# Block inversion in a hybrid decoder block: the order of the fp16 products on TensorE

## The chip, the core and the metric

The kernel runs on one core of a Trainium2 chip. The metric is the device time of one execution in microseconds (us). The engines of the core are written as in the profile: PE is TensorE's matmul side, PEld its weight loads, DVE is VectorE, ACT is ScalarE, POOL is GpSimd, SP is SyncE, which issues most transfers. Each engine works through its own queue in program order, and waits for the others at semaphores.

## The reference

One decoder layer over 512 tokens of width 2048. A projection of the normed input feeds two branches, RWKV-7 time mixing and sliding-window attention, which are gated, merged and followed by a gated ConvFFN. What matters here is the time mixing: each of 16 heads keeps a 64x64 state and updates it token by token.

```python
def step(state, inp):
    r_t, k_t, v_t, w_t, ka_t, kb_t = inp
    sa = jnp.einsum('bhvk,bhk->bhv', state, ka_t)
    state = (state * w_t[:, :, None, :] + sa[..., None] * kb_t[:, :, None, :]
             + v_t[..., None] * k_t[:, :, None, :])
    y = jnp.einsum('bhvk,bhk->bhv', state, r_t)
    return state, y
```

## The kernel before

The recurrence is computed in chunks of 64 tokens: 8 chunks, and the 16 heads in 8 pairs (two heads fill 128 partitions). Inside a chunk the updates `sa` depend on one another through a strictly triangular 64x64 matrix, so the kernel inverts a unit triangular matrix for each head and chunk. `late(p, st)` does this for pair p by block doubling: the loop over `LEVELS[1:]` takes m = 2, 4, 8, 16, 32, and each level has two products for all 8 chunks, called here the **A product** (left side `AI`, the matrix itself, right side `X`, the inverse so far) and the **B product** (left side `BT`, the transposed inverse so far, right side `IW`, which is made of the A product's result).

The products run in fp16, and for the accuracy each side is split into a high part (rounded to fp16) and a low part (the rest). `mm3(ps, wt, both, hi)` makes one product: the left side's parts `wt[:, 0]` (high) and `wt[:, 1]` (low) are the loaded weights, `both(n)` streams the high and the low right part of chunk n side by side (64 columns), `hi(n)` the high right part alone (32 columns). So a product is 16 matmuls with 16 weight loads: high left times both (L673) and low left times high (L674) for each chunk. One PSUM bank takes all chunks; `added` sums its two halves.

Between the two products of a level stands a chain over ACT and DVE: ACT copies one half of the sum out of PSUM (L686), DVE adds the other half (L687), DVE applies a mask (L697), ACT rounds the result into the high right part and DVE subtracts it for the low right part (both in `split`, L209 and L210). After the B product it goes on with L686, L687, L711, L712, the new parts of X (ACT L714, DVE L715) and the transposes of X into `BT` (PE L719, copied out by ACT and DVE in L723, two copies on each).

After the five levels a chain over the 8 chunks carries the state: PE L731, copied by DVE L732; PE L734 (with the inverse `BX` as weights), copied by ACT L735 and DVE L736; PE L740; DVE L744 updates the state for the next chunk. Then the group norm of the result follows (DVE L758 to L765, with a square on ACT, L762), and `final`, which starts with the transposes of PE L772.

All that time PE has other work to place between: `early(p + 1)`, the next pair's first steps, and the gates. They need six projection tiles for each pair, and every tile is 48 matmuls of 128x512 (`project`, L255 to L257: high times high, high times low, low times high), called **z matmuls** below. Their weights come by DMA into a ring of four tiles, are rounded by ACT (`whi`, L240) and subtracted by DVE (`wlo`, L241); a place in the ring comes free when PE has used the load that lay there four loads before. Per pair there are 288 z matmuls in all. In which order each engine does all this is not written in the code: outside the calls marked with `pin`, a list scheduler orders each engine's queue from its own estimates of durations, and a small change in one place moves instructions on all engines.

Of the kernel before, what the change touches and what calls it, by code (L numbers as in the profile page):

```python
# [23 lines left out]
NCH = S // C  # L24
# [110 lines left out]
def block_kernel(ctx: ExitStack, tc: tile.TileContext, d: Dims, a: dict, out: bass.AP):  # L135
    nc = tc.nc
    act, dve, pool, pe, sync = nc.scalar, nc.vector, nc.gpsimd, nc.tensor, nc.sync
# [140 lines left out]
    if True:  # L278
# [3 lines left out]
        with tc.tile_pool(name="x0_ps", bufs=6, space=PSUM) as ps0:  # L282
# [10 lines left out]
            for h in range(2):  # L293
                hs = slice(h * HT * P, (h + 1) * HT * P)
                for k in range(NK):
                    ps = ps0.tile([P, HT * P], F32, name="ps_x", tag="x")
# [45 lines left out]
        with ExitStack() as pt:  # L342
# [4 lines left out]
            def small():  # L347
                return mps.tile([P, S], F32, name="mi", tag="mi")
# [26 lines left out]
            for t in range(NKV):  # L375
# [12 lines left out]
                ps = small().rearrange("p (n c) -> p n c", c=P)  # L388
                for b in range(NT):
                    pe.transpose(ps[:, b], vf[:, b * P : (b + 1) * P], ident)  # L390
                ps = ps.rearrange("p n (h c) -> p n h c", c=HD)
# [14 lines left out]
            for g in range(NHK):  # L406
# [7 lines left out]
                for n in range(NT):  # L414
# [32 lines left out]
                    for kb in kbs:  # L447
                        ps = small().rearrange("p (h c) -> p h c", c=P)
# [3 lines left out]
                    ps = small()  # L452
                    for kb in kbs:
                        for i in range(2):
                            pe.matmul(ps, vhl[:, n - 1 + kb, g].rearrange("p e c -> p (e c)"),
                                      phl[i][:, kb].rearrange("p h c -> p (h c)"),
                                      start=kb == kbs[0] and i == 0, stop=kb == kbs[-1] and i == 1)
                    ol = ap_.tile([HD, S], F32, name="ol", tag="ol", bufs=2)
                    act.activation(ol, ps[HD:P], AF.Copy)
                    ps, ol = (x[0:HD].rearrange("p (e j c) -> p e j c", e=2, c=P) for x in (ps, ol))  # L460
# [6 lines left out]
        with ExitStack() as pr:  # L467
# [21 lines left out]
            def bulk():  # L489
                return blk.tile([P, S], F32, name="bulk", tag="bulk")  # L490
# [105 lines left out]
            def late(p, st):  # L596
# [23 lines left out]
                for n0 in range(0, NCH, 2):  # L620
                    ps = bulk()
# [8 lines left out]
                for g in range(2):  # L630
# [7 lines left out]
                    ps = bulk().rearrange("p (n c) -> p n c", c=P)  # L638
# [11 lines left out]
                for g in range(2):  # L650
# [4 lines left out]
                    ps = bulk().rearrange("p (n c) -> p n c", c=P)  # L655
# [3 lines left out]
                ps = bulk().rearrange("p (t c) -> p t c", c=P)  # L659
# [10 lines left out]

                def mm3(ps, wt, both, hi):
                    for n in range(NCH):
                        pe.matmul(ps[:, n], wt[:, 0, n], both(n), start=True, stop=False)  # L673
                        pe.matmul(ps[:, n, 0], wt[:, 1, n], hi(n), start=False, stop=True)  # L674

                def halves(m, t):

# [2 lines left out]
                def level_sum():  # L680
                    return bulk().rearrange("p (n e c) -> p n e c", e=2, c=HC)
# [8 lines left out]
                for m in LEVELS[1:]:  # L690
                    last = m == LEVELS[-1]
                    ps = level_sum()
                    cols = [halves(m, X[:, e]) for e in range(2)]
                    mm3(ps, AI, lambda n: X[:, :, n].rearrange("p e (b w m) -> p e b w m", w=2, m=m)[:, :, :, 1],
                        lambda n: cols[0][:, n])
                    tt = added(ps)
                    dve.tensor_tensor(tt, tt, mb(f"m{m}", NCH), op=ALU.mult)  # L697
                    split(IW[:, :, 0], IW[:, :, 1], tt)
                    if last:
                        for i, (lo, hi) in enumerate(HV):  # L700
# [3 lines left out]
                            else:  # L704
                                act.activation(own, own, AF.Copy, scale=1.0 / SG)
                    ps = level_sum()
                    mm3(ps, BT, lambda n: IW[:, n], lambda n: IW[:, n, 0])
                    sc = 1.0 / (SG * SG) if last else 1.0 / SG
                    tt = added(ps)
# [3 lines left out]
                    if not last:  # L713
                        act.activation(cols[0], tv, AF.Copy, scale=sc)  # L714
                        dve.scalar_tensor_tensor(cols[1], tv, sc, cols[0], op0=ALU.mult, op1=ALU.subtract)  # L715
                        ps = blk.tile([P, 2, NCH // 2, P], F16, name="bulk", tag="bulk")
# [11 lines left out]
                for n in range(NCH):  # L728
                    ps = chn.tile([P, 2, C], F32, name="psG", tag="chn")
# [3 lines left out]
                    ps = chn.tile([P, 2, C], F32, name="psU", tag="chn")  # L733
# [5 lines left out]
                    for h in (1, 0):  # L739
                        pin(pe.matmul(s2[:, n % HN, h], W2[:, n, 2 * h : 2 * h + 2].rearrange("p a c -> p (a c)"), UV[:, n, h],  # L740
                                      start=True, stop=True))
# [124 lines left out]
    with ExitStack() as pbb:  # L866
# [8 lines left out]
        for m, i in order:  # L875
            hi, lo, r0, n, gi = parts[i]
# [509 lines left out]
```

## Time and profile before

| | |
|---|---|
| three runs, median (lowest to highest) | 2829.64 us (2828.12 to 2833.07) |
| the profiled execution's own time | 2830.7 us |
| its span, from first to last instruction | 2828.9 us |
| TensorE's granted clock, mean | 0.996 |
| PE busy, weight loads busy | 2774.4 us (98%), 2403.0 us (85%) |
| DVE, ACT, POOL busy | 1987.5, 1342.1, 225.1 us |
| stretch with the eight pairs, 340 to 1080 us: PE busy | 730.92 of 740 us |

A busy PE is counted from a matmul's start to the modelled end of it, and matmuls overlap; so what PE loses in a place is read best from the starts of two matmuls that follow each other. In an answer of the timeline each row has the start, the duration, engine, line, operation and operands; in square brackets stands the time that the engine was idle before it, and who released it.

### The profile page before, as it was taken

The numbers are of one execution on the slowest core, as the hardware profiler recorded it, in microseconds if no ns is written. First come the engines' busy times: TensorE is split into PE (matmuls) and PEld (weight loads), VectorE is DVE, ScalarE is ACT, GpSimd is POOL, SyncE is SP. The second block draws the span as 40 slices with busy tenths as digits, with TensorE's granted clock in tenths as the row PEclk, the third lists the DMA queues.
The fourth block names the chain that finished last, engine by engine and source line by source line (L and its number), as shares of the span: only waits on it lengthen the run. The fifth ranks groups of instructions, "written<-read, shape, count | busy, mean of one in ns | idle before, by whom it ended". The sixth has DMA issues, their size and how long they took to land.

```text
span 2828.9 us, 45923 instructions
## 1 busy us (share of the span) xinstructions
PE 2774.4 (98%) x17450; PEld 2403.0 (85%) x17450; DVE 1987.5 (70%) x3437; ACT 1342.1 (47%) x2256; POOL 225.1 (8%) x299
## 2 busy tenths in 40 slices
PE   7999999999999999999999899999999999999999
PEld 5777777777777777888888899999999999888887
DVE  4588677777777774545678777878787878655555
ACT  4355445444544553322465455555545555444444
POOL 0001000000000001011010011011101110000000
PEclk9999999999999999999999999999999999999999
DMA  7865766666666667878777789888988897877775
GB/s 216 227 159 163 187 167 168 175 164 158 175 162 171 160 165 223 234 248 292 237 251 211 210 235 241 229 229 227 241 236 222 228 242 228 315 245 241 256 256 190
DMA packets 223726, 607.04 MB, mean 215 GB/s; under 512 B 24448, under 2 KB 44560, under 8 KB 222480
## 3 DMA queue, kind: packets, MB, share of 16 engines
q1 hardware_dynamic: 156096, 432.64, 47.1%
q0 software_dynamic: 36064, 132.14, 24.5%
q10 hardware_dynamic: 31344, 39.31, 4.0%
q8 instruction: 137, 2.24, 0.3%
q14 instruction: 85, 0.70, 0.1%
HBM read 554.38 MB, written 174.40 MB: 258 GB/s over the span
## 4 chain that ended last, share of the span: by engine, by line
PE 87%; DVE 5%; ACT 3%; DMA 2%; issue 1%; SPq 0%; POOL 0%; ACTq 0%; DVEq 0%; POOLq 0%
PE X L1087 18%; PE X L954 11%; PE acc L256 9%; PE acc L255 9%; PE acc L257 9%; PE Y L954 9%; PE Y L1087 9%; PE Z L1087 4%; DVE wlo L241 1%; PE psS L740 1%; PE psG L731 1%; PE bulk L623 1%; PE bulk L673 1%; PE bulk L534 1%; ACT whi L240 1%
## 5 line engine op out<-in xcount | busy, mean ns | idle before, releaser
L255 PE MATMUL acc<-xhi,whi 128*128 128x512 f32 x1152 | 462.9, 402 | 1.9 <-DVE xlo L301 1.9
L257 PE MATMUL acc<-xhi,wlo 128*128 128x512 f32 x1152 | 463.8, 403 | 0.0
L256 PE MATMUL acc<-xlo,whi 128*128 128x512 f32 x1152 | 462.2, 401 | 0.0
L947 DVE TENSOR_TENSOR wlo<-raw,whi 128x1024 fp32r<-128x1024 f32 x210 | 256.9, 1224 | 205.1 <-ACT whi L946 204.9
L240 ACT ACTIVATE whi<-raw 128x512 fp32r<-128x512 f32 x352 | 220.0, 630 | 375.7 <-PE acc L256 295.1
L946 ACT ACTIVATE whi<-raw 128x1024 fp32r<-128x1024 f32 x210 | 222.8, 1061 | 290.6 <-PE X L954 152.9
L241 DVE TENSOR_TENSOR wlo<-raw,whi 128x512 fp32r<-128x512 f32 x352 | 241.3, 689 | 167.1 <-ACT whi L240 146.9
L1087 PE MATMUL X<-b,whi 128*128 128x256 f32 x1472 | 270.2, 284 | 2.3 <-DVE u L1107 0.9
L1087 PE MATMUL X<-t,whi 128*128 128x256 f32 x1408 | 259.6, 285 | 10.3 <-DVE u L1107 9.8
L1070 DVE TENSOR_TENSOR wlo<-raw,whi 128x1024 fp32r<-128x1024 f32 x176 | 215.0, 1222 | 77.6 <-ACT whi L1069 77.3
L1087 PE MATMUL Y<-t,whi 128*128 128x256 f32 x1408 | 257.1, 283 | 0.0
L255 PEld LDWEIGHTS acc<-xhi,whi 128*128 128x128 f32 x1152 | 217.6, 189 | 43.4 <-issue 2.5
L256 PEld LDWEIGHTS acc<-xlo,whi 128*128 128x128 f32 x1152 | 217.5, 189 | 41.9 <-issue 3.3
L257 PEld LDWEIGHTS acc<-xhi,wlo 128*128 128x128 f32 x1152 | 217.5, 189 | 38.3 <-issue 1.1
L1069 ACT ACTIVATE whi<-a 128x1024 fp32r<-128x1024 f32 x132 | 139.3, 1056 | 216.5 <-DVE a L1063 214.3
L1087 PEld LDWEIGHTS X<-b,whi 128*128 128x128 f32 x1472 | 230.7, 193 | 3.1 <-issue 2.4
L1087 PEld LDWEIGHTS X<-t,whi 128*128 128x128 f32 x1408 | 221.6, 194 | 10.9 <-DVE u L1107 7.2
L1087 PEld LDWEIGHTS Y<-t,whi 128*128 128x128 f32 x1408 | 219.8, 192 | 0.0
L1087 PE MATMUL X<-b,wlo 128*128 128x256 f32 x736 | 209.3, 284 | 2.1 <-DVE wlo L1070 2.1
L1070 DVE TENSOR_TENSOR wlo<-a,whi 128x1024 fp32r<-128x1024 f32 x132 | 161.7, 1226 | 67.3 <-ACT whi L1069 66.7
L1087 PE MATMUL X<-t,wlo 128*128 128x256 f32 x704 | 200.4, 285 | 0.0
L1087 PE MATMUL Y<-t,wlo 128*128 128x256 f32 x704 | 199.4, 283 | 0.0
(339 smaller groups left out, 5762.1 us busy)
## 6 DMA issues: line engine op xcount, KB each, us to landing
raw<-in_w_up_dram SPq DMA_DIRECT2D x180, 512.0 KB, 4.6
raw<-in_w_z_dram SPq DMA_DIRECT2D x288, 256.0 KB, 3.9
s_dn<-in_w_dn_dram POOLq DMA_DIRECT2D x88, 512.0 KB, 5.9
raw<-in_w_up_dram POOLq DMA_DIRECT2D x88, 512.0 KB, 8.7
raw<-s_dn SPq DMA_DIRECT2D x88, 512.0 KB, 3.8
raw<-in_w_dn_dram SPq DMA_DIRECT2D x66, 512.0 KB, 3.5
a<-in_w_up_dram SPq DMA_DIRECT2D x48, 512.0 KB, 6.9
s_dn<-in_w_dn_dram SPq DMA_DIRECT2D x44, 512.0 KB, 4.9
```

The source lines that it names most:

```text
L240: act.activation(hi, raw, AF.Copy)
L241: dve.tensor_tensor(lo, raw, hi.bitcast(F32), op=ALU.subtract)
L255: pe.matmul(acc, whi[:, j], xhi[:, k], start=first, stop=False)
L256: pe.matmul(acc, whi[:, j], xlo[:, k], start=False, stop=False)
L257: pe.matmul(acc, wlo[:, j], xhi[:, k], start=False, stop=last)
L534: pe.matmul(ps, w[:, i], ads[:, i], start=i == lo, stop=i == hi - 1)
L946: act.activation(whi, wr, AF.Copy)
L947: dve.tensor_tensor(wlo, wr, whi.bitcast(F32), op=ALU.subtract)
L954: pe.matmul(dst, l[:, q, ts], r[:, es], start=fst and j == 0, stop=lst and j == 2, skip_group_check=True)
L1069: pin(act.activation(hi, t, AF.Copy))
L1070: pin(dve.tensor_tensor(lo, t, hi.bitcast(F32), op=ALU.subtract))
L1087: pin(pe.matmul(ps, l[:, k], r[:, k], start=start and k + i == 0, stop=last and i == 2, skip_group_check=True))
```

## The change

The loop over the chunks is split in two. First come the low left parts of all chunks times the high right part, then the high left parts times both. The first matmul of the product alone starts the accumulation, the last alone ends it.

```diff
                 def mm3(ps, wt, both, hi):
                     for n in range(NCH):
-                        pe.matmul(ps[:, n], wt[:, 0, n], both(n), start=True, stop=False)
-                        pe.matmul(ps[:, n, 0], wt[:, 1, n], hi(n), start=False, stop=True)
+                        pe.matmul(ps[:, n, 0], wt[:, 1, n], hi(n), start=n == 0, stop=False, skip_group_check=True)
+                    for n in range(NCH):
+                        pe.matmul(ps[:, n], wt[:, 0, n], both(n), start=False, stop=n == NCH - 1, skip_group_check=True)
```

In the changed file the low part's matmul is L673, the high part's L675, and every line behind it has a number higher by one. The number of matmuls, weight loads and columns is the same. The scheduler lays the queues out anew from the first pair's first A product on until the end of the last pair's state chain; before and behind that nothing moves. The three places below are from the fourth pair.

On PE, the B product at m = 16, before: the last two z matmuls ahead of it and its first chunk (AI and BT are the left sides, XIW the tile with X and IW, xhi, xlo, whi and wlo the parts of the projection).

```order
L257 MATMUL acc<-xhi,wlo 128x512
L255 MATMUL acc<-xhi,whi 128x512
L673 LDWEIGHTS BT
L673 MATMUL bulk<-XIW,BT 128x64
L674 LDWEIGHTS BT
L674 MATMUL bulk<-XIW,BT 128x32
```

And now, from the last of its low parts to the first of its high parts:

```order
L673 LDWEIGHTS BT
L673 MATMUL bulk<-XIW,BT 128x32
L256 MATMUL acc<-xlo,whi 128x512
L257 MATMUL acc<-xhi,wlo 128x512
L675 LDWEIGHTS BT
L675 MATMUL bulk<-XIW,BT 128x64
```

Before, the 16 matmuls stand in one block; now two z matmuls stand between the eight low and the eight high ones. It is so in every B product, with one to three z matmuls (at m = 32 the four matmuls of L327 stand there as well). The numbers of z matmuls between the A product and the B product of a pair, for the second to the seventh pair at m = 2, 4, 8, 16, 32, were 17 (and 8 more inside the A product), 14, 15, 11, 15, and are 13 (and 9 inside the A product), 11, 10, 11, 9. At m = 2 the A product stood in three pieces and stands in two. Behind the B product they were 13, 10, 12, 10 and are 10, 11, 10, 10, until the transposes of L719. In the state chain they were 87 and are 90, from there to the next pair's first product 76 and 85. The blocks of z matmuls of a pair were 38 and are 41 (in the last pair 35 and 39).

The same level on ACT, before, between the two products (XIW<-tt is the split's high part):

```order
L723 COPY BT<-bulk 64x8x64
L686 ACTIVATE tt<-bulk 128x256
L723 COPY BT<-bulk 64x8x64
L209 ACTIVATE XIW<-tt 128x8x32
L240 ACTIVATE whi<-raw 128x512
```

And now:

```order
L724 COPY BT<-bulk 64x8x64
L687 ACTIVATE tt<-bulk 128x256
L724 COPY BT<-bulk 64x8x64
L240 ACTIVATE whi<-raw 128x512
L209 ACTIVATE XIW<-tt 128x8x32
```

The rounding of a z weight has moved ahead of the split's high part. On DVE, before:

```order
L723 COPY BT<-bulk 64x8x64
L687 TENSOR_TENSOR tt<-bulk,tt 128x256
L697 TENSOR_TENSOR tt<-tt,cst 128x256
L723 COPY BT<-bulk 64x8x64
L210 TENSOR_TENSOR XIW<-tt,XIW 128x8x32
L241 TENSOR_TENSOR wlo<-raw,whi 128x512
```

And now:

```order
L724 COPY BT<-bulk 64x8x64
L688 TENSOR_TENSOR tt<-bulk,tt 128x256
L698 TENSOR_TENSOR tt<-tt,cst 128x256
L724 COPY BT<-bulk 64x8x64
L241 TENSOR_TENSOR wlo<-raw,whi 128x512
L210 TENSOR_TENSOR XIW<-tt,XIW 128x8x32
```

The subtraction for that z weight has moved ahead of the split's low part. Both moves are there at m = 4, 8 and 16 in the second to the eighth pair, and in the eighth at m = 32. Behind the B product at m = 4, in the same way, a `whi` now stands ahead of L711 and L714 on ACT, and its `wlo` ahead of L715 on DVE; behind the one at m = 2 they stood there before. In the first pair the queues of the two engines between the products are as before, but for a `whi` at m = 32.

At the state chain's first chunk the small steps of the next pair's norm (rq) stood on DVE, before, partly behind the copy of L736:

```order
L198 TENSOR_TENSOR rq_7060<-rq_7059 128x8
L736 COPY UV<-psU 64x64
L199 TENSOR_TENSOR rq_7060<-rq_7060,rq_7058 128x8
L200 SCALAR_TENSOR_TENSOR rq_7059<-rq_7060,rq_7059 128x8
L198 TENSOR_TENSOR rq_7060<-rq_7059 128x8
L199 TENSOR_TENSOR rq_7060<-rq_7060,rq_7058 128x8
L744 SCALAR_TENSOR_TENSOR SV<-SV,ee,psS 64x64 x2
```

And now:

```order
L713 TENSOR_SCALAR BX<-tt 64x8x32
L198 TENSOR_TENSOR rq_7060<-rq_7059 128x8
L199 TENSOR_TENSOR rq_7060<-rq_7060,rq_7058 128x8
L200 SCALAR_TENSOR_TENSOR rq_7059<-rq_7060,rq_7059 128x8
L198 TENSOR_TENSOR rq_7060<-rq_7059 128x8
L199 TENSOR_TENSOR rq_7060<-rq_7060,rq_7058 128x8
L737 COPY UV<-psU 64x64
L200 SCALAR_TENSOR_TENSOR rq_7059<-rq_7060,rq_7059 128x8
```

Five of these steps now stand between L713 and the copy of L737 (L712 and L736 before), and four more between that copy and the state's update. PE has 3 z matmuls between L734 and L740 there as before. Between L740 and L731 it had 4, and now has 2, the transpose L330 and one matmul of L558.

## Prediction

> **What bounds the kernel now.** I read the page's first lines, then the stretch of the eight pairs, then who waits for whom on the weight loader.
>
> ```profile
> span 2828.9 us, 45923 instructions
> PE 2774.4 (98%) x17450; PEld 2403.0 (85%) x17450; DVE 1987.5 (70%) x3437; ACT 1342.1 (47%) x2256; POOL 225.1 (8%) x299
> 340.00:1080.00 740.00, 730.92 (x4848) 581.26 (x4847) 553.28 (x1339) 357.82 (x795) 59.68 (x81) 1.00 0.67 166
> PEld L673 <- DVE XIW L210: 23.3, 40, 1.0
> PEld L719 <- DVE XIW L715: 8.3, 30, 0.4
> ```
>
> PE is the bound: it is busy for 730.92 of the 740 us in which the change acts. Whatever is won or lost here is time in which PE starts nothing, or starts something late. All 40 B products (8 pairs, 5 levels) wait for the low right part. What such a wait costs is read from the starts, here in the fourth pair at m = 16: on PE the last matmul of the A product, the z matmuls, the first two of the B product, and the B product's first weight load.
>
> ```profile
> 662.63 0.18 PE L674 MATMUL bulk<-XIW,AI 128*128 128x32 f16 x1
> 662.66 0.48 PE L257 MATMUL acc<-xhi,wlo 128*128 128x512 f32 x1
> 662.98 0.40 PE L255 MATMUL acc<-xhi,whi 128*128 128x512 f32 x1
> ...
> 664.80 0.39 PE L257 MATMUL acc<-xhi,wlo 128*128 128x512 f32 x1
> 665.03 0.39 PE L255 MATMUL acc<-xhi,whi 128*128 128x512 f32 x1
> 665.34 0.20 PE L673 MATMUL bulk<-XIW,BT 128*128 128x64 f16 x1
> 665.38 0.18 PE L674 MATMUL bulk<-XIW,BT 128*128 128x32 f16 x1
> ...
> 665.33 0.10 PEld L673 LDWEIGHTS <-BT 128*128 128x128 f16 x1 [0.34 <-DVE XIW L210]
> ```
>
> A z matmul takes 0.23 from start to start (664.80 to 665.03), the first one behind fp16 work 0.32 (662.66 to 662.98), an fp16 matmul 0.03. The B product came 0.31 after the last z matmul, so PE lost 0.08, while the loader shows 0.34 of idle: 0.26 of that is there without a wait. So the 23.3 us stand for 23.3 - 40 x 0.26 = 12.9 us of PE, 1.6 for each pair, and the 8.3 at L719 for 8.3 - 30 x 0.26 = 0.5. These 12.9 us are the most that the change can take away. What the chain between the products does in the same place, on ACT and then on DVE:
>
> ```profile
> 662.42 0.58 ACT L723 COPY BT<-bulk 64x512 f16<-64x512 f16 x1 [0.51 <-PE bulk L719]
> 662.90 0.38 ACT L686 ACTIVATE tt<-bulk 128x256 f32<-128x256 f32 x1
> 663.48 0.58 ACT L723 COPY BT<-bulk 64x512 f16<-64x512 f16 x1 [0.20 <-DVE BT L723]
> 664.40 0.42 ACT L209 ACTIVATE XIW<-tt 128x256 f16<-128x256 f32 x1 [0.33 <-DVE tt L697]
> 665.00 0.63 ACT L240 ACTIVATE whi<-raw 128x512 fp32r<-128x512 f32 x1 [0.19 <-PE acc L256]
> 663.03 0.42 DVE L723 COPY BT<-bulk 64x512 f16<-64x512 f16 x1 [0.40 <-ACT BT L723]
> 663.48 0.42 DVE L687 TENSOR_TENSOR tt<-bulk,tt 128x256 f32<-128x256 f32 x1
> 663.94 0.42 DVE L697 TENSOR_TENSOR tt<-tt,cst 128x256 f32<-128x256 f32 x1
> 664.40 0.43 DVE L723 COPY BT<-bulk 64x512 f16<-64x512 f16 x1
> 664.85 0.43 DVE L210 TENSOR_TENSOR XIW<-tt,XIW 128x256 f16<-128x256 f32 x1
> 665.66 0.69 DVE L241 TENSOR_TENSOR wlo<-raw,whi 128x512 fp32r<-128x512 f32 x1 [0.38 <-ACT whi L240]
> ```
>
> The high part is done at 664.82, the low part at 665.28; PE starts 0.06 after that. So the high part is there 0.46 earlier, which is the head start that the low left parts could use.
>
> **The change part by part.** *The product itself.* The same 16 matmuls and loads. A 64-column matmul and a 32-column one each take 0.03 to the next start, so I cost the new order at nothing; were the eight narrow ones packed at half of that, it would be 640 x 0.014 = 9 us less, and no row shows such a pitch.
>
> *The cover shrinks with the wait.* I count from the A product's last start, 662.63 above. n z matmuls let PE go on at 0.35 + (n - 2) x 0.23 + 0.24: 2.18 for 9, 2.41 for 10, 2.64 for 11. Then 8 x 0.03 = 0.22 for the low left parts, and with two z matmuls 0.32 + 0.24, so the high left parts are due 0.78 after the low ones began. On the other side, the BT copies end as before (DVE 2.20). At m = 16, ACT has its second copy behind it at 1.43 but then takes `whi` first, whose place in the ring comes free when the sixth z matmul ends (1.26 + 0.39 + 0.05 = 1.70): 1.70 to 2.33. ACT starts its next some 0.1 before an end (662.90 against 663.00), so the high part runs from 2.24 to 2.66 and PE has it at 2.72, 0.08 too late. DVE takes `wlo` from 2.38 to 3.07, the low part until 3.53; PE has it at 3.59, against 2.72 + 0.78 = 3.50, again 0.09 too late. That is 0.17 where 0.08 was lost. In the same way, m = 8 gives 0 for the high part (2.35 against 2.41) and 0.19 for the low (3.38 against 3.19); m = 4 some 0.05; m = 32 0.08 (2.26 against 2.18), with the low part behind L327. At m = 2 the fourth pair shows before:
>
> ```profile
> 641.94 0.39 PE L255 MATMUL acc<-xhi,whi 128*128 128x512 f32 x1
> 642.89 0.20 PE L673 MATMUL bulk<-XIW,BT 128*128 128x64 f16 x1 [0.56 <-DVE XIW L210]
> ```
>
> There 0.95 - 0.24 = 0.71 was lost. Now the product waits for a part that is ready 0.47 earlier, but with 22 z matmuls ahead of it for 25: 0.71 - 0.47 + 3 x 0.23 = 0.93. Behind the B products at m = 2 and 4, `whi` and `wlo` stand ahead of the new parts of X, and L719 gets some 0.2 of wait at each, where 0.5 / 8 = 0.06 stood in a pair. Sum for a pair: 0.93 + 0.05 + 0.19 + 0.17 + 0.08 + 0.4 = 1.8 against 1.6 + 0.06. So the wait does not go: the scheduler has taken away as much cover as the head start gives, and put weight splits into the gap. I take +0.15 a pair, +1.2 us for eight.
>
> *More blocks of z matmuls.* Each block's first costs 0.32 for 0.23. There are 3 more in seven pairs and 4 in the last: 25 x 0.09 = +2.3 us. The Trainium skill, in "TensorE: Matmul & The Clock Gate", section "Step-by-step: what each phase is for", says that the weight loads are pulled ahead of the matmuls in flight, so that the next tile's weights load while this tile's matmul runs. By that a new block would cost nothing and the sum be 2.3 less; the rows 662.66 and 662.98 differ from it, and I go by them.
>
> *The state chain.* At its first chunk, before (PE, ACT, then DVE):
>
> ```profile
> 676.31 0.38 PE L734 MATMUL psU<-GY,BX 128*128 128x128 f32 x2
> 677.27 0.66 PE L740 MATMUL psS<-UV,W 128*128 128x64 f32 x4
> 678.77 0.41 PE L731 MATMUL psG<-SV,BAR 128*128 128x64 f32 x2
> 676.73 0.22 ACT L735 ACTIVATE UV<-psU 64x64 f32<-64x64 f32 x1 [1.61 <-PE psU L734]
> 674.90 0.29 DVE L712 TENSOR_SCALAR BX<-tt 64x256 f32<-64x256 f32 x1
> 676.98 0.23 DVE L736 COPY UV<-psU 64x64 f32<-64x64 f32 x1 [0.98 <-ACT UV L735]
> 677.24 0.17 DVE L199 TENSOR_TENSOR rq<-rq,rq 128x8 f32<-128x8 f32 x1
> 677.45 0.17 DVE L200 SCALAR_TENSOR_TENSOR rq<-rq,rq 128x8 f32<-128x8 f32 x1
> 678.05 0.57 DVE L744 SCALAR_TENSOR_TENSOR SV<-SV,ee,psS 64x64 f32<-64x64 f32 x2
> ```
>
> Here DVE had been idle when L736 could start, 0.67 after L734. In the new order L712 releases L734, 0.29 + 0.06 after its own start, so L736 is wanted 0.35 + 0.67 = 1.02 after that start; but five rq steps of 0.2 each (677.24 to 677.45) stand between, and it starts at 0.3 + 5 x 0.2 = 1.3. L740 comes 0.3 late, and PE has only the three z matmuls for it that it had before. From L740 to L731 it takes 1.50, of which four z matmuls cover 0.32 + 3 x 0.23; two of them (0.46) are gone, and L330 and one L558 give some 0.3 back (three passes like L734's two, which take 0.38 to their end): 0.15 of wait. The four rq steps ahead of L744 end 0.23 + 0.8 after L736 begins, about when L744 could start (1.07), and cost nothing. Before, L740 came 0.27 after a z matmul, for 0.24, so next to nothing was lost. I take 0.45 and a little for the later chunks, 0.5 for each of the seven pairs that have a next one, +3.5 us; from 0, if L712 comes early enough behind the other work, to 1.0.
>
> *The norm behind it.*
>
> ```profile
> 707.19 0.66 PE L740 MATMUL psS<-UV,W 128*128 128x64 f32 x4
> 716.56 0.66 PE L772 MATMUL bulk<-ident,yc 128*128 128x128 f32 x4 [0.21 <-DVE yc L765]
> 711.53 0.63 ACT L762 ACTIVATE gn<-yc 128x512 f32<-128x512 f32 x1 [1.07 <-DVE yc L760]
> 712.19 0.69 DVE L763 TENSOR_REDUCE st<-gn 128x8 f32<-128x512 f32 x1 [0.70 <-ACT gn L762]
> 715.81 0.69 DVE L765 TENSOR_TENSOR yc<-yc,rg 128x512 f32<-128x512 f32 x1
> ```
>
> L772 waits for L765 already. Two more z matmuls (39 for 37) cover 0.46, but one `whi` now stands ahead of L762 and one more `wlo` among the steps between L763 and L765 (0.69, as in the row 665.66). I take +0.15 a pair, +1.0 us, between -2.5 (the cover alone) and +4.
>
> *The sum.* 1.2 + 2.3 + 3.5 + 1.0 = 8.0 us on the profiled execution's own 2830.7 us (span 2828.9 and 1.8 around it): 2838.7. The median of the three runs is 1.1 lower; by that 2837.6.
>
> **The rivals.** *The head start is kept whole* (the other side). If the cover is enough in spite of the moves, the 12.9 us go and only the 2.3 for the blocks come: 2829.6 - 12.9 + 2.3 = 2819. For it: the high part is 0.46 early at every level, and the low one is then covered by the low left parts and the z matmuls behind them. Against: the z matmuls ahead of the product went down by 3 to 6 at four of the five levels. It decides at 0.46 / 0.23: with two z matmuls less the gain is gone.
>
> *Nothing but the blocks.* The waits of the levels, the chain and the norm stay as they were in sum: 2829.6 + 2.3 = 2832. For it: the same work, and PE has 288 z matmuls a pair to hide the chain with. Against: the rq steps on DVE.
>
> *The high part is held up on ACT.* `whi` waits for its place in the ring, and L209 stands behind it. At m = 16 the place comes free at 1.70 and ACT could have taken it at 1.33; each z matmul by which it comes later puts 0.23 on the product. With two more in the 22 products that have the `whi` there, 22 x 0.46 = 10 us on top: 2848.
>
> *The blocks are free.* The first z load could run under the fp16 matmuls ahead of it, and its matmul take 0.23 like the others: 2837.6 - 2.3 = 2835.3. Against it stand the rows 662.66 and 662.98. The rule of the Trainium skill given above would make it so.
>
> That the change does nothing is no case of its own: the queues are in another order.
>
> **How the numbers follow.** About 0.2% (5.7 us) is what a measurement of this kernel can tell from no change, so "same" is 2824 to 2835.3. Chances: my forecast 0.55, nothing but the blocks 0.18, blocks free 0.05 (half of it same), held up on ACT 0.10, head start kept 0.12. The forecast's own spread, by the ends of the chain and the norm, is 2831 to 2844, and about a fifth of it is same. Slower: 0.55 x 0.8 + 0.025 + 0.10 = 0.57; same: 0.11 + 0.18 + 0.025 = 0.31; faster: 0.12. The range leaves out the head start kept whole and the far half of the hold-up, 0.17 together: 2827 to 2847.
>
> **What would show it.** Right: PE's waits at the low left parts for ACT L209 and at the high left parts for DVE L210 together above 12 us by the starts; 25 more first z matmuls at 0.32; L740 (then L741) late at the first chunk behind the rq steps; the stretch of the pairs about 748 us, 743 at least. Wrong: a B product that goes on without wait at m = 2, the stretch of the pairs under 738 us, or more than 6 us found outside it.

## The result, and the profile after

| | before | after |
|---|---|---|
| median (lowest to highest) | 2828.88 us (2826.98 to 2833.07) | 2844.38 us (2841.20 to 2850.88) |
| ratio of the two, 95% interval | | 1.0053 (1.0041 to 1.0065) |
| profiled execution | 2830.7 us | 2841.2 us |

The changed kernel is slower, by 15.5 us between the medians and 10.5 between the two profiled executions. Five later runs of it, taken with the experiments, gave 2841.94 beside 2830.26, so +11.7. The top of the page of after, and then its stretch of the eight pairs as the prediction read it (PE, PEld, DVE, ACT, POOL busy, PE's clock, share and rate of the transfers):

```profile
span 2839.4 us, 45940 instructions
PE 2784.7 (98%) x17450; PEld 2404.9 (85%) x17450; DVE 1986.4 (70%) x3437; ACT 1337.8 (47%) x2256; POOL 225.4 (8%) x299
```

```profile
340.00:1080.00 740.00, 729.81 (x4796) 573.45 (x4795) 547.71 (x1327) 352.23 (x791) 58.98 (x80) 1.00 0.66 164
```

The clock is the same, and PE is as busy, but in the same 740 us it got through 4796 matmuls instead of 4848. How long the eight pairs take is read from the first pair's L661 to the last pair's first transpose for `final`. PE in the timeline of before, then of after:

```profile
342.01 0.66 PE L661 MATMUL bulk<-ident,vz 128*128 128x128 f32 x4
1103.83 0.66 PE L772 MATMUL bulk<-ident,yc 128*128 128x128 f32 x4 [0.19 <-DVE yc L765]
```

```profile
341.26 0.66 PE L661 MATMUL bulk<-ident,vz 128*128 128x128 f32 x4
1112.85 0.66 PE L773 MATMUL bulk<-ident,yc 128*128 128x128 f32 x4 [0.19 <-DVE yc L766]
```

That is 761.8 against 771.6 us: 9.8 of the 10.5 us lie in the pairs. This "pairs' time" moves little from run to run, while the 339 to 343 us ahead of it and the 1720 to 1728 behind it vary by some us each (the last section shows what the latter goes with), so I compare the experiments by it as well as by their medians.

The B product at m = 2 of the fourth pair, which lost 0.71 before. On PE, after (the rows of the eight low and of the eight high matmuls are merged):

```profile
645.43 0.39 PE L255 MATMUL acc<-xhi,whi 128*128 128x512 f32 x1
646.64 0.35 PE L673 MATMUL bulk<-XIW,BT 128*128 128x32 f16 x8 [0.81 <-ACT XIW L209]
646.84 0.47 PE L256 MATMUL acc<-xlo,whi 128*128 128x512 f32 x1
647.15 0.40 PE L257 MATMUL acc<-xhi,wlo 128*128 128x512 f32 x1
647.39 0.41 PE L675 MATMUL bulk<-XIW,BT 128*128 128x64 f16 x8
```

It now waits for ACT's high part, and longer: 1.21 from the last z matmul, of which 0.24 would be there anyway, so 0.97. The high parts (L675) wait for nothing. At m = 16 of the same pair almost nothing is lost, 0.02 and then 0.04:

```profile
667.48 0.39 PE L255 MATMUL acc<-xhi,whi 128*128 128x512 f32 x1
667.74 0.35 PE L673 MATMUL bulk<-XIW,BT 128*128 128x32 f16 x8
667.94 0.47 PE L256 MATMUL acc<-xlo,whi 128*128 128x512 f32 x1
668.25 0.39 PE L257 MATMUL acc<-xhi,wlo 128*128 128x512 f32 x1
668.52 0.39 PE L675 MATMUL bulk<-XIW,BT 128*128 128x64 f16 x8
```

Counted in this way over all 40 B products, PE lost 12.6 us before and loses 9.3 now. The first chunk of the fourth pair's state chain, after (PE, ACT, DVE):

```profile
677.83 0.46 PE L735 MATMUL psU<-GY,BX 128*128 128x128 f32 x2
679.00 0.66 PE L741 MATMUL psS<-UV,W 128*128 128x64 f32 x4
678.33 0.22 ACT L736 ACTIVATE UV<-psU 64x64 f32<-64x64 f32 x1 [0.67 <-PE psU L735]
678.51 0.17 DVE L199 TENSOR_TENSOR rq<-rq,rq 128x8 f32<-128x8 f32 x1
678.71 0.23 DVE L737 COPY UV<-psU 64x64 f32<-64x64 f32 x1
```

DVE goes straight from the rq step into the copy L737; L741 comes 1.17 after L735, where it came 0.96 after it before. And one thing that no step of the prediction had, in the second pair (who waited on PE in the whole run: total, times, longest; then the chain of waits around it):

```profile
PE psU L735 <- DVE GY L733: 1.4, 1, 1.4
```

```profile
481.69 0.20 DVE rsT L332
481.88 0.02 issue
481.90 2.50 DMA rsd<-rsT
...
484.47 0.48 SPq L338
484.95 0.05 issue
485.00 6.38 DMA rsb<-rsd
491.38 0.03 issue
491.41 0.02 DVEq L552
491.43 0.04 issue
491.48 0.69 DVE kk L552
```

The next pair's norm goes out to DRAM and comes back spread over the partitions, 9.5 us in all. DVE's L552 needs it, and in the new order L552 stands ahead of a copy GY L733 of the state chain, so DVE and then PE stood still; PE lost 1.5 us by the starts.

### The profile page after: what moved, and what is told of

Its sections match the earlier page's. It is cut to its first block, busy times and chain, and to the rows that moved or that the text cites. A ratio compares the mean times of both kernels' runs of the same rounds, so it can differ in the third digit from the quotient of the medians.

```text
span 2839.4 us, 45940 instructions
## 1 busy us (share of the span) xinstructions
PE 2784.7 (98%) x17450; PEld 2404.9 (85%) x17450; DVE 1986.4 (70%) x3437; ACT 1337.8 (47%) x2256; POOL 225.4 (8%) x299
## 4 chain that ended last, share of the span: by engine, by line
PE 89%; DVE 4%; DMA 2%; ACT 2%; issue 1%; ACTq 0%; SPq 0%; POOL 0%; DVEq 0%; POOLq 0%
PE X L1088 17%; PE X L955 11%; PE acc L256 10%; PE acc L257 10%; PE acc L255 10%; PE Y L955 9%; PE Y L1088 8%; PE Z L1088 4%; PE psS L741 1%; PE psG L732 1%; PE bulk L623 1%; DMA raw<-in_w_up_dram 1%; DMA raw<-in_w_dn_dram 1%; PE bulk L675 1%; PE bulk L534 1%
```

## The experiments

To part the product's order from the queues that the scheduler made for it, most of these kernels carry a table with the order of every engine's queue, of before or of after, and chain each engine's instructions in it. An edit of the table is shown as the rows that it moves. All medians stand beside runs of the kernel before on the same chip (2829.87, 2830.12 and 2830.26 in the three groups); the lost time at B products and the blocks are counted from the starts.

| kernel | median us | ratio to before, 95% | pairs' time | lost at B products |
|---|---|---|---|---|
| new_order_old_queues | 2822.79 | 0.9976 (0.9966 to 0.9986) | 755.0 | 4.6 |
| old_order_new_queues | 2865.31 | 1.0128 (1.0114 to 1.0142) | 796.1 | 35.4 |
| low_first_by_chunk | 2831.03 | 1.0003 (0.9993 to 1.0012) | 764.5 | 6.1 |
| low_first_but_two | 2822.66 | 0.9973 (0.9962 to 0.9983) | 755.0 | 5.3 |
| but_two_own_queues | 2842.03 | 1.0040 (1.0028 to 1.0053) | 773.4 | |
| z_ahead_of_low | 2835.29 | 1.0026 (1.0017 to 1.0035) | 768.3 | 10.2 |
| kk_behind_gy | 2841.88 | 1.0044 (1.0030 to 1.0058) | 776.1 | |
| rq_behind_uv | 2842.87 | 1.0043 (1.0030 to 1.0055) | 775.3 | |
| kk_spread | 2845.17 | 1.0050 (1.0038 to 1.0063) | 779.7 | |
| all_three | 2848.77 | 1.0057 (1.0044 to 1.0070) | 778.3 | |
| after_again | 2841.94 | 1.0044 (1.0032 to 1.0057) | 776.6 | |
| kk_no_trip | 2837.26 | 1.0024 (1.0015 to 1.0033) | 770.2 | 9.3 |

**The order, the queues, and each without the other.** The changed code in the queues of before; of the table only the first pieces of the A product at m = 2 move:

```diff
 PE, A product at m = 2, second to last pair (in the first, three z matmuls stand in place of the five)
-low 0 to 3, low 4 to 7, z z z, high 0, z z z z z, high 1 to 7
+low 0 to 3, z z z z z z z z, low 4 to 7, high 0 to 7
```

> The changed code, but every engine's queue is chained in the order of before; only in the A product at m = 2 the four low parts of the later chunks stand behind the z matmuls that stood in it, and in each product the 16 places hold the low parts first. Theory 1, the loss comes from the re-laid queues and the product's own order gains: the five B products' waits of before (0.71, 0.33, 0.29, 0.07, 0.25 us in the fourth pair) shrink by up to 0.22 each, the time of eight low parts, so by at most 0.95 a pair and 7.6 us in all: 2821 to 2827. Rival, the order of the 16 matmuls itself costs (the two waits, the accumulation across chunks): 2835 or more. Rival, it does nothing, since the low parts wait for the same thing: 2828 to 2831.

And the code of before in the queues of after, nothing moved:

> The code of before, but every engine's queue is chained in the order of the changed kernel; the 16 matmuls hold high and low part of each chunk in turn. Theory 1, the re-laid queues are the loss, and the product's order takes some of it back: slower than the changed kernel, since the first matmul then needs the subtracted low right part too (up to 0.7 us more at each B product): 2847 to 2860. Rival, the order of the 16 matmuls is the loss: back to 2828 to 2834.

Theory 1 held on both sides, though the second time lies 5 us above its range. In the old queues the new order is 7.1 us faster than before; in the new queues the old order is 35 us slower than before. PE in new_order_old_queues, m = 2 and then m = 16 of the fourth pair:

```profile
637.99 0.39 PE L255 MATMUL acc<-xhi,whi 128*128 128x512 f32 x1
638.37 0.35 PE L673 MATMUL bulk<-XIW,BT 128*128 128x32 f16 x8
638.85 0.39 PE L675 MATMUL bulk<-XIW,BT 128*128 128x64 f16 x8
...
660.41 0.39 PE L255 MATMUL acc<-xhi,whi 128*128 128x512 f32 x1
660.64 0.36 PE L673 MATMUL bulk<-XIW,BT 128*128 128x32 f16 x8
660.86 0.39 PE L675 MATMUL bulk<-XIW,BT 128*128 128x64 f16 x8
```

At m = 16 the product follows the z matmul without a gap and its high parts follow the low ones: the 0.08 of before is gone. At m = 2, 0.71 has become 0.14 ahead of the low parts and 0.28 between low and high. Over all B products 12.6 us became 4.6, a gain of 1.0 a pair, about the 0.95 that was expected at the most; 1.2 us of it went back into the low parts of the A product at m = 2. Who waits in old_order_new_queues:

```profile
PE bulk L673 <- DVE XIW L210: 29.3, 40, 1.4
```

All 40 B products wait again for DVE's low part, 35.4 us by the starts. So the new queues are laid out for a product that can begin without the low part: the order takes 24.5 us off the pairs' time there (796.1 to 771.6) and 6.8 in the old ones, and the queues cost 34.3 with the old order and 16.6 with the new one.

**Is it the eight low parts that run ahead?** The queues of before, and the product in one loop:

```diff
                     for n in range(NCH):
                         pe.matmul(ps[:, n, 0], wt[:, 1, n], hi(n), start=n == 0, stop=False, skip_group_check=True)
-                    for n in range(NCH):
                         pe.matmul(ps[:, n], wt[:, 0, n], both(n), start=False, stop=n == NCH - 1, skip_group_check=True)
```

> The queues of before, and the product in one loop: low part of a chunk, then its high part, chunk by chunk (the first matmul of the product alone starts the accumulation, the last alone ends it). If the 7 us of new_order_old_queues come from the seven or eight low parts that run while DVE still subtracts: here only one low part runs ahead of the first matmul that needs the subtraction, 0.03 us at each of 40 products, 1.2 us in all: 2827.5 to 2830.5. Rival, they come from a matmul that waits for ACT alone and lets the weight loads and the next matmuls in, or from the accumulation across chunks: 2821 to 2825.

The time came out a little above the range expected, and the traces say why. Who waits on PE, and the place in the fourth pair (PE, then DVE):

```profile
PE bulk L673 <- DVE AI L210: 8.0, 8, 1.1
```

```profile
636.98 0.40 PE L257 MATMUL acc<-xhi,wlo 128*128 128x512 f32 x1
638.44 0.19 PE L673 MATMUL bulk<-XIW,AI 128*128 128x32 f16 x1 [1.07 <-DVE AI L210]
637.71 0.68 DVE L210 TENSOR_TENSOR AI<-at__6516,AI 128x512 f16<-128x512 f32 x1
```

In the A product at m = 2 the second four chunks' low left part is the last thing that DVE writes; before, a high left part stood in this place, which was there earlier. That costs 1.46 - 0.23 = 1.23 a pair, 9.2 us in all. The delay also hides the wait of the B product at m = 2 (0.71). At m = 4 to 32 the fourth pair lost 0.28, 0.24, 0.06 and 0.22 instead of 0.33, 0.29, 0.07 and 0.25: 0.03 or so less at each, one narrow matmul. With eight of them ahead it was 0.11, 0.04, 0 and 0.04. So the gain is that of the low parts run ahead, and not of the accumulation across chunks. low_first_but_two, also in the untouched queues of before, takes the product in the new order but for that one place:

```diff
+                ALL = [(n, low) for low in (1, 0) for n in range(NCH)]
+                TWO = [(n, low) for n0, low in ((0, 1), (0, 0), (4, 0), (4, 1)) for n in range(n0, n0 + 4)]
...
-                    mm3(ps, AI, ..., lambda n: cols[0][:, n])
+                    mm3(ps, AI, ..., lambda n: cols[0][:, n], TWO if m == 2 else ALL)
```

> The queues of before, untouched, and the new order in all products but the A product at m = 2: there the first four chunks come with their low parts, then their high parts, and after the z matmuls the last four with their high left parts first, since AI's low part for these is the last thing that DVE writes (in low_first_by_chunk PE waited 1.23 us there in every pair, in new_order_old_queues 0.17). It takes those 0.17 us a pair away and may add a little to the wait of the next B product: 2820.5 to 2823.5. Rival, the wait only moves to that B product, as the scheduler's cover there is thin: 2823 to 2826.

The wait at the A product is gone, but the B product behind it has 0.09 more (0.23 for 0.14 in the fourth pair), and each pair has one block of z matmuls more than in new_order_old_queues, so the pairs' time is the same 755.0. The median lies in the first range, but half of the wait moved, as the rival says. These two are the versions that beat both kernels; they can't be told apart. The same code without the table:

> The code of low_first_but_two, but the scheduler lays the queues out anew. If the loss of the changed kernel comes from the scheduler's answer to any order that lets the product begin earlier: 2836 to 2848. Rival, it came of the A product at m = 2 alone, whose pieces it had to re-lay: 2820 to 2832.

It lies where the changed kernel lies (773.4 in the pairs, with two stalls as that at 491 us). The scheduler's answer is the loss, whichever of the two orders it is given.

**Which part of the new queues costs it?** Four edits of the queues of after. First, the z matmuls that stand inside the B products are put ahead of them:

```diff
 PE, each B product
-low 0 to 7, z (one to three), high 0 to 7
+z (one to three), low 0 to 7, high 0 to 7
```

> The changed kernel with its own queues, but the one to three z matmuls between the low and the high parts of each B product stand ahead of the low parts (at m = 32 the four matmuls of L327 stay between). 32 blocks of z matmuls fewer. If a block's first z matmul costs 0.09 us more than the others: 2.9 us less, of which the high parts give back what the z matmuls covered of the wait for DVE's subtraction, 0.1 to 0.3 us at each product whose low parts waited for ACT (two or three a pair): between 1 us faster and 4 us slower than the changed kernel, and the first z matmuls behind other matmuls still take 0.32 us from start to start. If blocks cost nothing: 2 to 7 us slower.

By the medians it is far better than expected, 9.1 us under the changed kernel's first four runs and 6.7 under the later five. Between the two profiled executions it is 5.9 us, of which 3.3 lie in the pairs (771.6 to 768.3, each profile with one stall as that at 491 us). There it has 40 blocks of z matmuls fewer (not 32: those at m = 32 moved too), at 0.087 each 3.5 us, and loses 0.9 more at the B products. The other 2.6 lie outside the pairs, where nothing was moved, 2.3 of them behind the pairs, where the granted clock differs (last section). How the larger distance of the medians is made up, no profile shows; it may hold stalls. Second, the rq steps:

```diff
 DVE, first chunk of the state chain, second to seventh pair
-L198 L199 L200 L198 L199 L737 L200 L198 L199 L200 L745 L745
+L198 L737 L199 L200 L198 L199 L745 L745 L200 L198 L199 L200
```

> The changed kernel with its own queues, but on DVE four of the small steps of rsqrt (L198 to L200), which the new order put ahead of the first copy UV L737 of the state chain, stand behind it, and the next four behind the state's update L745, as before, in the second to the seventh pair. If these steps are what makes the chain later (the prediction's term of 3.5 us; the first L741 waits 0.17 us in each pair of the changed kernel and did not before): 3 to 6 us less, 2838 to 2842. Rival, the chain is later because fewer z matmuls stand between its steps: within 1.5 us of the changed kernel, and L741 still waits.

L741 then came without the 0.17, but the matmul that needs the rq steps' result came late instead. PE and DVE in the fourth pair:

```profile
678.91 0.17 DVE L200 SCALAR_TENSOR_TENSOR rq<-rq,rq 128x8 f32<-128x8 f32 x1
679.13 0.27 PE L330 MATMUL bulk<-ident,rq 128*8 128x128 f32 x1 [1.03 <-DVE rq L200]
```

In new_order_old_queues L330 stands further back on PE, behind the second chunk's L735. The pair became 0.9 us longer than in the changed kernel. So neither side of the expectation held: the rq steps do make L741's wait, which is about 1 us over six pairs, but the edit says nothing on the rest of the chain's price. Third, L552, in two ways:

```diff
 DVE, second to seventh pair: kk_behind_gy
-L552 L733 L587 L241 L737
+L733 L552 L587 L241 L737
 kk_spread (and on PE the matmul L591 behind the next L732)
-L552 L733 L587 L241 L737 L589 L745 L745 L751 L751 L593 L733
+L733 L552 L737 L241 L587 L745 L745 L589 L733 L751 L751 L593
```

> The changed kernel with its own queues, but on DVE the multiplication L552 (kk by rsb, which comes back through DRAM) stands behind the copy GY L733 that followed it, as it did before, in the second to the seventh pair. Theory 3, the round trip through DRAM sometimes comes late and, from its place ahead of GY, stops the state chain (1.5 us once in the profile of the changed kernel): 2838 to 2843, and the runs lie within 4 us of each other, as those of before. Rival, the spread of the changed kernel's runs (2841 to 2851) has another source: 2842 to 2846 with the same spread.

> The changed kernel with its own queues, but L552 (kk by rsb) stands behind the copy GY L733, and what hangs on it (L587, L589, the matmul L591, L593) is spread behind the copies and updates that follow, so that no chain step stands behind two of them; in kk_behind_gy the stall had only moved to the next L741 (0.72 us, and 1.0 and 1.25 where the transfer came late). Theory 3, the late transfer from its place ahead of GY makes the changed kernel's stalls and spread: no stall of over 0.3 us at L735 and L741 in any pair, 2839 to 2842.5, spread at most 5 us. Rival, they only move once more: a wait of 0.5 us or more at another step of the chain, 2841 to 2845.

Both took the stall away from L735 and put another in its place. In kk_behind_gy it is the copy L737 that stands behind too much; DVE and PE, third pair:

```profile
590.70 0.69 DVE L552 TENSOR_TENSOR kk<-kk,rsb 128x512 f32<-128x512 f32 x1 [0.32 <-DMA rsb<-rsd]
592.75 0.23 DVE L737 COPY UV<-psU 64x64 f32<-64x64 f32 x1
593.03 0.66 PE L741 MATMUL psS<-UV,W 128*128 128x64 f32 x4 [0.85 <-DVE UV L737]
```

In kk_spread it is the state's update L745 behind L587, and L732 waits 0.7 for it in each of the six pairs (1.0 in the fourth, where the transfer came late). Its runs are close together (2842.78 to 2846.16), as those of kk_behind_gy (2839.70 to 2843.60), so a nearly fixed loss took the place of a changing one. Of kk_spread's pairs' time 1.6 us are no wait: for 3.4 us of the fourth pair PE's granted clock was 0.5.

> The changed kernel with its own queues and three edits together: the z matmuls ahead of the low parts (z_ahead_of_low: 9.1 us less), the small steps of rsqrt behind the copies (rq_behind_uv), L552 and what hangs on it spread (kk_spread). If the loss sits in these three places the sum holds, 9 and 1 to 3 and 0 to 6: 2826 to 2834, and the rest to the 2822.8 of the new order in the old queues is the waits at L720 and L773 and in the first pair. Rival, each edit makes another wait last: 2834 to 2838.

The rival's mechanism held, and the time lies even above its range: the new waits at L330 and L732 are both there, and the pairs' time is 778.3. So none of these moves alone carries the loss of the new queues, and which of their moves is worth what stays open. Counted from the starts between the changed kernel without its stalls (770.2, below) and new_order_old_queues (755.0), 33 more blocks at 0.087 are 2.9 us and the products' waits 3.5. Of the other 8.8 us, 5.7 lie in the state chain (its time less 0.228 for every z matmul, 0.087 for every block and 0.108 for every matmul of L327) and 1.3 are waits at L720; no run isolates them. The chain's part is 0.9 in each of the second to the seventh pair, 0.3 in the first, and nothing in the eighth, which has no next pair's work among its steps.

**The stalls.** The changed kernel once more, and beside it the same queues with an L552 that waits for no transfer:

```diff
-                dve.tensor_tensor(kk, kk, rb, op=ALU.mult)
+                dve.scalar_tensor_tensor(kk, kk, 0.0, thw, op0=ALU.mult, op1=ALU.mult)
```

> The changed kernel as it is, for its spread beside kk_no_trip. Theory 3 (late transfers ahead of GY): a median of 2841 to 2847, runs up to 10 us apart, and where the profile has a stall of over 1 us in the state chain, DVE's L552 waits for the transfer into rsb. Rival, the first four runs were spread by chance: 2839 to 2843, at most 5 us apart.

> The changed kernel in its own queues, but L552 multiplies kk by zero and by a resident tile, so that it no longer waits for the norm's round trip through DRAM (the transfers still run; what is left out is that kk is divided by its norm, so all that follows from kk is zero). Theory 3: the seven pairs after the first take 99.0 us each with no stall at L735, and the runs lie within 5 us of each other, 2838 to 2843. Rival, the spread comes from outside the pairs (the first 340 us and the last 1727 us): as spread as the changed kernel beside it, and the same median within 1.5 us.

Who waited in after_again, and then in kk_no_trip:

```profile
PE psU L735 <- DVE GY L733: 4.8, 4, 1.9
DVE kk L552 <- DMA rsb<-rsd: 11.1, 5, 4.4
```

```profile
PEld psU L735 <- DVE GY L733: 1.7, 7, 0.2
```

In this profile of the changed kernel four of six pairs have the stall, 1.5, 1.5, 2.1 and 0.4 us by the starts, and its pairs' time is 776.6; in the first profile it was one, and 771.6. Without the wait there is none, the pairs after the first take 99.04 to 99.16 us each, and the sum is 770.2. Theory 3 holds for the pairs. The median of kk_no_trip lies 0.7 us under its range, and its runs still spread over 7 us (2833.14 to 2840.31) where 5 were expected, so the stalls are not all of the spread. The slowest of these runs is the profiled one, which has no stall, so the rest lies outside the pairs; the runs of before spread as much (2825 to 2835).

## Why the prediction was right, and where not

The sign and the range came out, and the profiled execution lies 2.5 us above its forecast (2841.2 for 2838.7). The first four runs' median is 6.8 above (2844.4 for 2837.6), the later five's 4.3. The sum was +8.0, and the pairs' time without the stalls went up by 770.2 - 761.8 = 8.4. That these two agree is luck: counted in the same way as above, the levels between the first A product and the chain gave 0.0 where 1.2 were forecast, the blocks 2.2 for 2.3, the state chain 5.7 for 3.5, the norm 0.5 for 1.0, so the errors cancel. What the stalls add to it was in no term.

- *The wait moves to ACT's high part and stays as long.* This step failed. At m = 2 the hand count gave 0.93 and 0.97 was measured. At m = 16 it gave 0.17 and 0.06 came: I had let DVE's `wlo` take 0.69 there, and the next step began 0.60 after its start. (Its formula also gives 2.20, 2.43 and 2.66 for 9, 10 and 11 z matmuls, 0.02 more than written.) The sum over all B products fell from 12.6 to 9.3 us. "Above 12" is refuted, and it did not follow from the prediction's own terms: 0.93 + 0.05 + 0.19 + 0.17 + 0.08 = 1.42 a pair is 11.4 us for eight. L720 took 0.28 in the fourth pair where I had 0.4.
- *The product itself costs nothing.* So far right, but a product in the new order is worth 7 us in the old queues and 24.5 in the new ones. The rival that the head start is kept whole (2819) comes near to new_order_old_queues at 2822.8, where the waits fell to 4.6 us and not to nothing. What spoke against it, that the scheduler takes cover away, is part of the reason why it doesn't show in the changed kernel (9.3 us there); the state chain is the larger part.
- *25 more blocks at 0.09.* Held: 326 blocks against 301, a first z matmul 0.315 and the others 0.228 or 0.229 from start to start (medians), so 2.2 us. The Trainium skill ("TensorE: Matmul & The Clock Gate", "Step-by-step: what each phase is for") says that the next tile's weights load while this tile's matmul runs; that a new block would therefore cost nothing, as the prediction drew from it, the traces do not bear out for the first z matmul of a block.
- *The state chain, 0.5 a pair.* The place was right, the size too small. L741 at the first chunk waits 0.17 (0.3 predicted) and the L732 behind it 0.16 (0.15 predicted), but the chain as a whole took 0.86 more in the fourth pair: three of its later steps wait 0.05 to 0.07 as well, and between the four matmuls of each L741 it is 0.26 more over the eight chunks.
- *The norm, 0.15.* Measured 0.05 in the fourth pair.
- *Not foreseen:* L552 ahead of GY. It stood in the new order for everyone to see, 9.5 us of transfers behind a place in DVE's queue that the state chain needs; I had looked at that stretch of DVE for the rq steps alone. It is 1.5 us by the starts in one profile of the changed kernel and 5.5 in the other.

## What to carry to other kernels

Where two parts of a product come ready one after the other, run all matmuls that need the first part, then those that need both: the gain is the time of the matmuls run ahead, at most the wait that stands there, and one operand that comes late for another reason (here AI's low part) turns it round. Where a scheduler lays out the queues, cost the code and the queues apart: keep the old queues and put the new code in, and the new queues with the old code. Here the list scheduler spent the head start at once on less cover. And look in a new order for every instruction that waits for a transfer: ask what is queued behind it.

## What was not expected of the hardware

The way of the norm's row through DRAM (4 KB out, two reads of 128 KB back) changes in length from pair to pair. SP's issue of the read and DVE's L552 in after_again, in the longest and the shortest case in which L552 waited:

```profile
786.15 1.29 SPq L338 DMA_DIRECT2D rsb<-rsd  x2
793.96 0.69 DVE L552 TENSOR_TENSOR kk<-kk,rsb 128x512 f32<-128x512 f32 x1 [2.40 <-DMA rsb<-rsd]
...
889.04 1.12 SPq L338 DMA_DIRECT2D rsb<-rsd  x2
893.68 0.69 DVE L552 TENSOR_TENSOR kk<-kk,rsb 128x512 f32<-128x512 f32 x1 [0.68 <-DMA rsb<-rsd]
```

From issue to use it took 7.8 us in the one and 4.6 in the other, in the same queues. The read was issued 2.4 us after the end of the row's copy (DVE L332) in the one and 3.8 after it in the other, so from that copy to the use it was 10.2 and 8.5. Why the lengths differ stays open.

The time behind the pairs follows PE's granted clock, which stands at 0.5 for 3.4 us, or two or three times that, at a few places of each execution. The stretch from 1500 to 1600 us in after and then in but_two_own_queues (behind the five busy times: clock, share and rate of the transfers):

```profile
1500.00:1600.00 100.00, 87.61 (x671) 86.63 (x670) 76.61 (x91) 50.52 (x65) 7.89 (x11) 0.90 0.73 200
1500.00:1600.00 100.00, 86.84 (x703) 85.45 (x702) 81.22 (x99) 53.85 (x71) 9.85 (x14) 0.97 0.77 218
```

Behind the pairs the first took 1726.6 us and the second 1720.4, with the half clock for 20.5 and 6.8 us. All fourteen profiles go this way: 1720.4 and 1721.3 with 6.8 us of it, 1722.7 and 1723.4 with 10.2, 1724.3 to 1725.1 with 13.7, 1726.5 to 1727.9 with 17.1 or 20.5. What sets the clock is not shown.

The order of the queues weighs more than that of the product: the same instructions took 2822.8 or 2844.4 us with the new order, 2829.9 or 2865.3 with the old.
